# Light-part products over 128 zero-filled rows instead of 64 in a two-block transformer kernel

## The chip, the cores and the metric

The kernel runs on one core of one Trainium2 chip, as one launch. The metric is the device time of that launch in microseconds (us), as the median of three runs. All operands are in float32 in memory; the large products run in float32r passes on TensorE.

## The reference, cut to what matters

The reference is a chain of two blocks over 512 tokens of 1024 features (16 learned tokens are put ahead of them in the first block). Three places of it matter here.

- RWKV-7 time mixing: `w_log = -softplus(-(w0 + tanh(xw @ w1) @ w2)) - 0.5` and `a = sigmoid(a0 + (xa @ a1) @ a2)`. The latents `tanh(xw @ w1)` and `xa @ a1` have 64 features each.
- Stick-breaking attention over 16 heads of 64 features: `z = einsum('bhqd,bhkd->bhqk', q, k) * scale`, then `w = exp(log_sigmoid(z) + log_after)` for the valid keys, where `log_after` sums `log_sigmoid(-z)` over the keys between this one and the query, and then `w @ v`.
- Window attention with 16 query heads and 4 key-value heads of 64 features, over a band of 512 tokens and 256 context tokens: `s = einsum('bkgqd,bkjd->bkgqj', q, k) * hd**-0.5`, a masked softmax with a sink, and `p @ v`.

Around them stand two feed-forward layers per block, a short convolution and the norms; they take most of the time and aren't touched.

## The kernel before, in words

Everything is feature-major: features lie on the 128 partitions, tokens along the free axis. A float32 product is made of float32r products: an operand x is split in a heavy part (x rounded to float32r) and a light part (the rest), and `W.T x` becomes heavy times heavy, heavy times light, light times heavy. `Net.load_split` does this for weights (`whi` on ACT, L82, and `wlo` on DVE, L83), `Net.split` for data (L170 and L171, or L173 and L174 with a scale), and the loop of L131 issues the products of all dense layers.

Heads and latents have 64 features, so their operands fill half the partitions. The kernel stacks two parts there: one 128-row product covers heavy times heavy on 64 rows and light times heavy on the other 64. What is left, heavy times light, is a second product over the 64 rows of the head alone. This is the product the change touches, in three stages:

- `latents` (inside `rwkv`, L521 to L533): for 8 feature tiles, two latents and two halves of the tokens, a product over 128 rows (L529, operand `lh`) and one over 64 rows (L530, operand `ll`), then a Tanh on ACT into a tile of the pool `ew` and a store to DRAM. The steps alternate by hand with steps of `project` (L608), the projections.
- `scores` (inside `stick`, L1228): for each of 8 feature tiles, two heads and three PSUM banks, one to three regions of keys and queries; for each region a 128-row product and a 64-row product through the helper `mm` (L1223, `z<-qd,ks` and `z<-ql,ks`). DVE and ACT make the softplus of a bank; `weights` (also L1223, `s<-...`) sums it, `values` (L1294) multiplies with the values. The loop at L1347 runs 48 turns; scores are issued three turns ahead (AHEAD), and four steps of dense products, the generator `stream` with `project(j)` for the keys (`ev_k`), queries (`ev_q`) and values (`ev_v`) of the next feature tile, fill each turn. The query tiles `qd` and `ql` have one buffer.
- `softmax` (inside `window`, L1713): for 4 key-value heads and 4 query blocks, four heads with two products each over 128 rows (L1726) and 64 rows (L1727), 256 or 320 columns wide, in a PSUM tile `s` of a pool with two buffers. DVE takes the maximum (L1732) and a small minimum (L1734), ACT the exponential (L1736), which is the last reader of `s`. `values` (L1746) transposes and multiplies (L1753, L1762). Five steps of dense products (`fill`, `part`) are issued with each of the 16 turns.

Before that loop `window` makes keys and queries: `normed` (L1587) takes a projection, its mean square (L1593), the rotation (L1596, `t` on DVE in L1598, two POOL products L1599 and L1600), the inverse root (`Net.rsqrt`, L179 to L183, into `r`) and the last product by `r` (L1603). Its scratch comes from the pool `wq` with two buffers per tag; `ev_k` (L1606) then fills `kh` and `kl`, `ev_q` the stacked queries.

The order on each engine's queue is fixed when the program is built: the framework walks the instructions by priority (their order in the program) and by when its own estimates say their operands and buffers are ready, and adds the waits. A tile of a pool waits until the tile that had its buffer before has been read for the last time.

Of the kernel before, what the change touches and what calls it, by code (L numbers as in the profile page):

```python
"""Block of RWKV-7 and stick-breaking attention followed by a block of window attention and short convolution,
feature-major: features on partitions, tokens along the free axis."""
# [6 lines left out]
F32 = mybir.dt.float32  # L9
F32R = mybir.dt.float32r  # L10
BF16 = mybir.dt.bfloat16
AF = mybir.ActivationFunctionType
ALU = mybir.AluOpType
# [6 lines left out]
T1 = 528  # L20
# [7 lines left out]
class Vecs:  # L28
    """Column offsets of per-feature vectors packed as [128, n]."""
# [19 lines left out]
class Net:  # L49
# [18 lines left out]
    def load_split(self, srcs, n, shape=None):  # L68
        """Streams a weight chunk of n columns per partition and splits it in two float32r parts. It is one source, or
        with a shape (rows k of the partition) several, side by side."""  # L70
# [19 lines left out]
    def steps(self, xs, W, K, tiles, T, evac, gsz, psum, tag="slot", first=False, last=False):  # L90
        """Generator, a step for each 128 rows of W: out[tile] = W[:, tile].T @ x for 128-column tiles, in three float32r passes.
        T = 512: one bank per tile; otherwise the tokens lie as halves in two banks. With first, the first group
        takes the tokens in two halves, x(k, half); with last, the last one ends with one half, and evac gets
        (tile, psum, tokens)."""
# [4 lines left out]
        for gi, grp in enumerate(groups):  # L99
# [38 lines left out]
            # the halves of a tile are one group of a bank when both are open at once  # L138
# [20 lines left out]
    def squares(self, pool, name, names, tag="cst"):  # L159
        """Constant [128, 128] matrices by name."""  # L160
# [5 lines left out]
    def split(self, hi, lo, src, scale=None, bias=None):  # L166
        """hi + lo = src * scale + bias, both float32r."""
# [8 lines left out]
    def rsqrt(self, out, m, t):  # L176
        """out = m ** -0.5 with one Newton step; t is scratch."""
# [8 lines left out]
class Norm:  # L186
    """rs = 1/sqrt(mean square + eps) of each token, on all partitions, in two halves of the tokens. Squares are
    taken of src * weight where there are weights (columns of squared weights)."""
# [44 lines left out]
def halved(tc, T, mk, fill, prep=None):  # L233
    """x(k), x(k, half): the parts of operand k, made at their first use by fill(k, hi, lo, tokens)."""
# [22 lines left out]
def ffn1(net, l, h, skip):  # L257
    """Block 1: h += W_down(silu(gate) * val), causal conv of the up projection; h: 8 tiles of tokens, of which
    the first skip only feed the convolution (0: zeros precede the tokens)."""
# [65 lines left out]
R1, R2 = 0.58, 1.11  # L325
DENSE = (77, 90, 44, 38)
PAT = "cdpcddcpddcd"
# time of a side generator's wait, in units of its own
LAG = 1.57


# [1539 lines left out]
```

## Time and profile before

| what | value |
|---|---|
| median of 3 runs | 3076.61 us |
| lowest and highest | 3064.46 and 3077.65 us |
| span of the profiled execution, first to last instruction | 3064.8 us |
| TensorE (PE) busy | 2982.8 us, 97% |
| weight loads (PEld) busy | 2501.0 us, 82% |
| DVE, ACT, POOL busy | 1782.9, 1373.8, 372.6 us |

The profile shows one execution, of which no time outside its span is given; its span lies 11.8 us below the median of the runs and 0.3 us above the lowest. A matmul's busy time includes the tail in which the next one already runs, so the distance between the starts of two matmuls says what one costs in a stream, not its duration. PEld are the loads of the stationary operand, which are separate instructions. PEclk is the granted clock as a share of 2.4 GHz.

### The profile page before, as it was taken

To read this page: it belongs to the slowest core of one execution; us is meant where nothing else is said; L and a number is where in the kernel's file an instruction comes from. 1 tells how busy PE (TensorE), PEld (TensorE's weight loads), DVE (VectorE), ACT (ScalarE), POOL (GpSimd) and SP (SyncE) were. 2 spreads that over 40 slices of the span, in tenths; PEclk is the share of its full clock that TensorE was granted. 3 is DMA by queue.
4 is the path that set the end of the run, shared out by engine and by line. 5 is a ranking of instruction groups with operands and counts; after the bars stand their busy time and mean duration, and the time that the engine had idled before them with its cause. 6 is when DMAs were issued, how large, how long until landed. Compare 5 with 4: busy or idle time off the path is not lost.

```text
span 3064.8 us, 51007 instructions
## 1 busy us (share of the span) xinstructions
PE 2982.8 (97%) x21232; PEld 2501.0 (82%) x21232; DVE 1782.9 (58%) x2833; ACT 1373.8 (45%) x2416; POOL 372.6 (12%) x394
## 2 busy tenths in 40 slices
PE   6989999989999999999999999999999999999999
PEld 3877776779999988889999886668888888888888
DVE  6677557456664377675666377765555344365532
ACT  6554534444443267774443156554443232343431
POOL 2323324210000000000000111101111100101100
PEclk9999999989999999999999999999999999999999
DMA  4335456322222221112222331002232223223232
GB/s 132 124 111 157 156 185 197 112 91 83 90 91 90 85 70 45 46 42 90 90 90 90 96 108 56 21 8 69 90 97 93 93 90 94 92 90 95 91 100 86
DMA packets 269543, 286.28 MB, mean 93 GB/s; under 512 B 12384, under 2 KB 243936, under 8 KB 269312
## 3 DMA queue, kind: packets, MB, share of 16 engines
q1 hardware_dynamic: 269312, 283.03, 29.2%
q8 instruction: 166, 2.72, 0.4%
q14 instruction: 65, 0.53, 0.1%
HBM read 271.70 MB, written 11.29 MB: 92 GB/s over the span
## 4 chain that ended last, share of the span: by engine, by line
PE 76%; DVE 1%; ACT 1%; issue 0%; DVEq 0%; ACTq 0%
PE slot L131 65%; PE z L1223 2%; PE s L1223 1%; PE s L1727 1%; PE po L1762 1%; PE pt L1753 1%; PE s L1726 1%; PE po L1294 1%; PE psn L215 1%; PE s L1729 1%; PE psh L1593 0%; PE psr L1596 0%; ACT whi L82 0%; PE psd L1768 0%; DVE wlo L83 0%
## 5 line engine op out<-in xcount | busy, mean ns | idle before, releaser
L131 PE MATMUL slot<-xh,whi 128*128 128x264 f32 (+3 forms) x2848 | 783.7, 324 | 2.6 <-ACT xh L1439 1.9
L131 PE MATMUL slot<-xh,wlo 128*128 128x264 f32 (+3 forms) x2848 | 777.0, 322 | 1.4 <-DVE wlo L83 1.4
L131 PE MATMUL slot<-xl,whi 128*128 128x264 f32 (+3 forms) x2848 | 777.4, 321 | 0.7 <-DVE xl L1440 0.7
L82 ACT ACTIVATE whi<-raw 128x1024 fp32r<-128x1024 f32 x368 | 382.6, 1040 | 830.2 <-PE slot L131 700.8
L83 DVE TENSOR_TENSOR wlo<-raw,whi 128x1024 fp32r<-128x1024 f32 x368 | 447.9, 1218 | 511.1 <-ACT whi L82 507.2
L131 PEld LDWEIGHTS slot<-xh,whi 128*128 128x128 f32 x2848 | 481.1, 189 | 54.4 <-issue 8.7
L131 PEld LDWEIGHTS slot<-xl,whi 128*128 128x128 f32 x2848 | 482.4, 190 | 44.4 <-issue 1.5
L131 PEld LDWEIGHTS slot<-xh,wlo 128*128 128x128 f32 x2848 | 480.8, 189 | 45.0 <-DVE wlo L83 1.6
L131 PE MATMUL slot<-mh,whi 128*128 128x512 f32 (+2 forms) x1012 | 291.0, 327 | 0.8 <-DVE h L1489 0.5
L131 PE MATMUL slot<-ml,whi 128*128 128x512 f32 (+2 forms) x1012 | 291.3, 327 | 0.0
L131 PE MATMUL slot<-mh,wlo 128*128 128x512 f32 (+2 forms) x1012 | 291.1, 327 | 0.0
L200 POOL TENSOR_TENSOR acc<-acc,sq 128x512 f32<-128x512 f32 (+2 forms) x40 | 67.0, 1674 | 1130.9 <-ACT sq L205 743.5
L131 PEld LDWEIGHTS slot<-mh,whi 128*128 128x128 f32 x1012 | 173.9, 188 | 19.9 <-DVE h L1489 0.9
L131 PEld LDWEIGHTS slot<-mh,wlo 128*128 128x128 f32 x1012 | 174.1, 189 | 18.2
L131 PEld LDWEIGHTS slot<-ml,whi 128*128 128x128 f32 x1012 | 173.6, 188 | 18.1
L1478 POOL TENSOR_TENSOR t<-t 128x512 f32<-128x512 f32 x44 | 75.3, 1711 | 460.9 <-DVE t L1456 425.0
L289 DVE TENSOR_TENSOR u<-slot,rs 128x528 f32<-128x528 f32 (+1 forms) x88 | 61.6, 702 | 109.0 <-PE slot L131 108.1
L170 ACT ACTIVATE mh<-t 128x512 fp32r<-128x512 f32 (+1 forms) x88 | 55.6, 632 | 145.5 <-POOL t L1478 78.8
L608 PE MATMUL slot<-xl,whi 128*128 128x264 f32 x384 | 110.0, 306 | 10.2 <-DVE xl L582 6.1
L608 PE MATMUL slot<-xh,whi 128*128 128x264 f32 x384 | 117.3, 326 | 1.4 <-ACT V L611 0.7
L608 PE MATMUL slot<-xh,wlo 128*128 128x264 f32 x384 | 106.5, 298 | 0.0
L171 DVE TENSOR_TENSOR ml<-t,mh 128x512 fp32r<-128x512 f32 (+1 forms) x88 | 60.9, 694 | 57.5 <-ACT mh L170 55.7
(415 smaller groups left out, 4889.2 us busy)
## 6 DMA issues: line engine op xcount, KB each, us to landing
aw<-in_ada_w SPq DMA_DIRECT2D x96, 512.0 KB, 3.9
raw<-in_ffn_up SPq DMA_DIRECT2D x88, 512.0 KB, 3.5
raw<-in_ffn_w_up SPq DMA_DIRECT2D x80, 512.0 KB, 3.4
raw<-in_ffn_down SPq DMA_DIRECT2D x40, 512.0 KB, 3.4
raw<-in_ffn_w_down SPq DMA_DIRECT2D x40, 512.0 KB, 3.4
raw<-in_sc_w_in SPq DMA_DIRECT2D x20, 512.0 KB, 3.4
raw<-in_win_w_qkv SPq DMA_DIRECT2D x12, 512.0 KB, 3.6
h<-in_xT SPq DMA_DIRECT2D x16, 264.0 KB, 4.6
```

Of the source, the lines that this page charges most:

```text
L82: nc.scalar.activation(hi[:, :n], raw[:, :n], AF.Copy)
L83: nc.vector.tensor_tensor(lo[:, :n], raw[:, :n], hi[:, :n].bitcast(F32), op=ALU.subtract)
L131: self.nc.tensor.matmul(out(j, i), a, b if i is None else b[:, i * H:i * H + H], start=(k == 0 and p == 0 and not (i and shared)), stop=(k ...
L170: nc.scalar.activation(hi, src, AF.Copy)
L171: nc.vector.tensor_tensor(lo, src, hi.bitcast(F32), op=ALU.subtract)
L200: nc.gpsimd.tensor_tensor(self.acc, self.acc, sq, op=ALU.add)
L215: add = lambda a, **kw: nc.tensor.matmul(ps[:, :N], self.net.ones, a, **kw)
L289: nc.vector.tensor_tensor(u[:, 2:].rearrange("p (a t) -> p a t", a=2), p, rs3, op=ALU.mult)
L608: nc.tensor.matmul(s[:, :264], a[:, c], b[:, halves[hf]], start=k == n == 0, stop=k == 7 and n == 2)
L1223: nc.tensor.matmul(out, a, x, **kw)
L1294: nc.tensor.matmul(po[hp(e), lo:hi], vt[:, b, hp(e)], w(e)[:, c + lo - t0:c + hi - t0], start=B == 0 and b == 2, stop=B == 2 and hi == 512)
L1478: nc.gpsimd.tensor_tensor(t, t, gate[j], op=ALU.mult)
```

## The change

Each 64-row product becomes a product over all 128 rows. The heavy operand with both stacked parts is already there on 128 rows; the light operand gets a tile of its own per head with zeros on the other 64 partitions, written by POOL memsets, so that the sum is the same.

- `latents`: `ll` becomes two tiles, one of them new, with a memset of 64 x 528 each.
- `stick`: `ql` becomes [128, 2, 516] with two memsets of 64 x 516 for each feature tile. The scratch `kf` of `ev_k` and `ev_q` goes from two buffers to one.
- `window`: `kl` becomes four tiles instead of two, with four memsets of 64 x 768. In `normed` the tag `r` is gone: `r` takes its buffer from the tag `hr`, which the rotation's `t` uses too.

```diff
-        ll, gh, gl, g3 = (room[:, i] for i in range(4))
+        gh, gl, g3 = (room[:, i] for i in range(3))
+
+        ll = [room[:, 3], tp.tile([128, T1], F32R, name="ll")]
         for r in range(2):
-            net.split(lh[r][hp(r)], ll[hp(r)], lat[hp(r)])
+            nc.gpsimd.memset(ll[r][hp(1 - r)].bitcast(F32), 0.0)
+            net.split(lh[r][hp(r)], ll[r][hp(r)], lat[hp(r)])
             nc.scalar.activation(lh[r][hp(1 - r)], lat[hp(r)], AF.Copy)
...
-                        nc.tensor.matmul(s[:, :264], w2[r][hp(r), js], ll[hp(r), c], start=False, stop=True)
+                        nc.tensor.matmul(s[:, :264], w2[r][:, js], ll[r][:, c], start=False, stop=True)
...
-            kf = t2.tile([128, T1], F32, tag="kf", name="kf")
+            kf = t2.tile([128, T1], F32, tag="kf", name="kf", bufs=1)
...
-            qf = t2.tile([128, T1], F32, tag="kf", name="qf")[:, :TQ]
+            qf = t2.tile([128, T1], F32, tag="kf", name="qf", bufs=1)[:, :TQ]
             qd = t2.tile([128, 2, TQ], F32R, tag="qd", name="qd", bufs=1)
-            lo = t2.tile([128, TQ], F32R, tag="ql", name="ql", bufs=1)
+
+            ql = t2.tile([128, 2, TQ], F32R, tag="ql", name="ql", bufs=1)
             nc.vector.tensor_tensor(h3(qf), p, h3(rs[:, Q0:]), op=ALU.mult)
             for e in range(2):
                 own, other = hp(e), hp(1 - e)
-                net.split(qd[own, e], lo[own], qf[own], 0.125)
+                net.split(qd[own, e], ql[own, e], qf[own], 0.125)
                 nc.scalar.activation(qd[other, e], qf[own], AF.Copy, scale=0.125)
-            ops["q", j] = (qd, lo)
+                nc.gpsimd.memset(ql[other, e].bitcast(F32), 0.0)
+            ops["q", j] = (qd, ql)
...
-                mm(z[:, c:c + w], ks[hp(e), e, kb], ql[hp(e), q], start=False, stop=True)
+                mm(z[:, c:c + w], ks[:, e, kb], ql[:, e, q], start=False, stop=True)
...
-        kl = [big.tile([128, 768], F32R, name=f"kl{i}") for i in range(2)]
+        kl = [big.tile([128, 768], F32R, name=f"kl{i}") for i in range(4)]
...
+        for i, t in enumerate(kl):
+            nc.gpsimd.memset(t[hp(1 - i % 2)].bitcast(F32), 0.0)
...
-            s, sq, m, r = (wq.tile([128, T2], F32, tag=t, name=t)[:, :T] for t in ("hq", "sq", "m", "r"))
+
+            s, sq, m = (wq.tile([128, T2], F32, tag=t, name=t)[:, :T] for t in ("hq", "sq", "m"))
...
             nc.vector.tensor_scalar(m, ps[:, :T], 1.0 / 64, 1e-6, op0=ALU.mult, op1=ALU.add)
+            r = wq.tile([128, T2], F32, tag="hr", name="hr")[:, :T]
             net.rsqrt(r, m, sq)
...
-                    nc.vector.tensor_tensor(kl[t][hp(e), d], n[hp(e), c], k[hp(e), d].bitcast(F32), op=ALU.subtract)
+                    nc.vector.tensor_tensor(kl[2 * t + e][hp(e), d], n[hp(e), c], k[hp(e), d].bitcast(F32), op=ALU.subtract)
...
-                    nc.tensor.matmul(o, q[r, qc], kl[kvh // 2][r, ks], start=False, stop=not mk)
+                    nc.tensor.matmul(o, q[:, qc], kl[kvh][:, ks], start=False, stop=not mk)
```

## Rows read from the trace of the kernel before

**Rows 1.** The head of the profile's page: the span, then busy time, share and instructions of each engine.

```profile
span 3064.8 us, 51007 instructions
PE 2982.8 (97%) x21232; PEld 2501.0 (82%) x21232; DVE 1782.9 (58%) x2833; ACT 1373.8 (45%) x2416; POOL 372.6 (12%) x394
```

**Rows 2.** Busy time by stretch. A row has the stretch (us from the span's start), its length, then busy us and number of instructions of PE, PEld, DVE, ACT and POOL, the granted clock, the share of the DMA engines and GB/s. The first row is the stretch of the latents and the second a part of it, then the stick-breaking attention, the start of the window attention, and the window attention's loop.

```profile
58.00:95.00 37.00, 35.65 (x149) 25.80 (x149) 11.18 (x14) 23.62 (x51) 5.24 (x5) 0.82 0.35 124
60.00:73.00 13.00, 13.00 (x40) 9.58 (x41) 6.55 (x7) 9.87 (x20) 4.04 (x3) 0.50 0.29 104
...
1091.00:1365.00 274.00, 273.96 (x1888) 234.44 (x1887) 191.11 (x330) 201.00 (x353) 3.07 (x13) 0.99 0.16 46
1820.00:1866.00 46.00, 39.74 (x188) 30.33 (x187) 37.56 (x53) 34.11 (x64) 11.90 (x8) 0.93 0.26 77
1866.00:2075.00 209.00, 208.55 (x1114) 132.00 (x1114) 142.77 (x308) 116.92 (x262) 23.85 (x27) 1.00 0.07 21
```

**Rows 3.** The light-part products of the three stages, from the views of their lines: number, shortest, median and longest duration in ns, first and last start, rows x columns of the stationary operand, shapes of the moving one.

```profile
L530 PE MATMUL slot<-room x32: 279/385/586, 59.0 to 94.6; 64*128 64x264 f32 x32
...
L1223 PE MATMUL z<-ql,ks x96: 268/386/699, 1092.0 to 1350.3; 64*128 64x272 f32 x16, 64*128 64x144 f32 x16, 64*128 64x16 f32 x16, 64*128 64x400 f32 x16
...
L1727 PE MATMUL s<-kl,q x128: 378/394/413, 1866.9 to 2073.1; 64*128 64x256 f32 x64, 64*128 64x320 f32 x64
```

**Rows 4.** PE in order of time, dense products alone: first start, time to the last end, engine, line, operation, tile, shapes and number. Six of 512 columns in a row, then a row of products of 264 columns, two per entry; of each series the first and the last.

```profile
1922.51 0.39 PE L131 MATMUL slot<-xh,whi 128*128 128x512 f32 x1
...
1923.67 0.40 PE L131 MATMUL slot<-xh,wlo 128*128 128x512 f32 x1
...
1203.29 0.41 PE L131 MATMUL slot<-xl,whi 128*128 128x264 f32 x2
...
1205.23 0.28 PE L131 MATMUL slot<-xh,whi 128*128 128x264 f32 x1
```

**Rows 5.** PE in order of time in the window attention: a pair of 320 columns and what follows it, then one of 256 columns and what follows it.

```profile
1899.72 0.39 PE L1726 MATMUL s<-kh,q 128*128 128x320 f32 x1
1900.04 0.41 PE L1727 MATMUL s<-kl,q 64*128 64x320 f32 x1
1900.39 0.23 PE L1729 MATMUL s<-masks 128*128 128x128 bf16 x1
...
1924.46 0.36 PE L1726 MATMUL s<-kh,q 128*128 128x256 f32 x1
1924.75 0.38 PE L1727 MATMUL s<-kl,q 64*128 64x256 f32 x1
1925.06 0.38 PE L1726 MATMUL s<-kh,q 128*128 128x256 f32 x1
```

**Rows 6.** The weight loads (PEld) in order of time in the same attention; in brackets the idle time before the load and what ended it.

```profile
1901.63 0.18 PEld L1727 LDWEIGHTS s<-kl,q 64*128 64x128 f32 x1 [0.15 <-issue]
```

**Rows 7.** PE in order of time in the stick-breaking attention: the first product of a unit of bank 0 (three pairs) and the product after the unit, the same for a unit of bank 1 (two pairs) and of bank 2 (one pair).

```profile
1201.36 0.39 PE L1223 MATMUL z<-qd,ks 128*128 128x272 f32 x1
...
1202.94 0.39 PE L131 MATMUL slot<-xh,whi 128*128 128x264 f32 x1
...
1146.47 0.45 PE L1223 MATMUL z<-qd,ks 128*128 128x400 f32 x1
...
1147.62 0.38 PE L131 MATMUL slot<-xl,whi 128*128 128x258 f32 x1
...
1150.52 0.48 PE L1223 MATMUL z<-qd,ks 128*128 128x512 f32 x1
...
1151.35 0.40 PE L131 MATMUL slot<-xh,whi 128*128 128x258 f32 x1
```

**Rows 8.** PE in order of time in the latents: the first of two pairs and the product after them.

```profile
83.29 0.28 PE L529 MATMUL slot<-room 128*128 128x264 f32 x1
...
84.45 0.39 PE L608 MATMUL slot<-xh,whi 128*128 128x264 f32 x1
```

**Rows 9.** Two heads of the window attention in order of time: the first score product on PE and the exponential on ACT that reads the same PSUM tile last.

```profile
1931.14 0.39 PE L1726 MATMUL s<-kh,q 128*128 128x256 f32 x1
...
1934.10 0.69 ACT L1736 ACTIVATE P<-s,st 128x512 f32<-128x512 f32 x1 [0.41 <-DVE st L1734]
...
1938.30 0.71 PE L1726 MATMUL s<-kh,q 128*128 128x320 f32 x1
...
1944.42 0.80 ACT L1736 ACTIVATE P<-s,st 128x640 f32<-128x640 f32 x1 [2.20 <-DVE st L1734]
```

**Rows 10.** ACT, DVE and PE in order of time at the start of the window attention, for a pair of key tiles and then a pair of query tiles: the second tile's write of `r`, the first tile's last read of its `r`, and the next wait of PE.

```profile
1830.84 0.63 ACT L179 ACTIVATE r<-m 128x512 f32<-128x512 f32 x1 [0.43 <-DVE m L1601]
...
1835.23 0.68 DVE L1603 TENSOR_TENSOR hq<-hq,r 128x512 f32<-128x512 f32 x1
...
1844.03 0.39 PE L131 MATMUL slot<-ch,whi 128*128 128x256 f32 x1 [3.30 <-ACT whi L82]
...
1851.32 0.63 ACT L179 ACTIVATE r<-m 128x512 f32<-128x512 f32 x1
...
1856.08 0.68 DVE L1603 TENSOR_TENSOR hq<-hq,r 128x512 f32<-128x512 f32 x1
...
1858.55 0.53 PE L131 MATMUL slot<-ch,wlo 128*128 128x256 f32 x1 [2.10 <-DVE wlo L83]
```

**Rows 11.** POOL: a memset by form (number, busy us, mean ns of one, idle us before them and what ended it), and its longest wait in the stick-breaking attention (us in total, times, longest).

```profile
L710 POOL MEMSET w<- 128x448 f32 x4 | 1.9, 475 | 5.4 <-PE slot L544 5.3
...
POOL vf L1185 <- PE psv L1197: 158.4, 7, 31.0
```

More of the change, by code (lines that the diff above doesn't have):

```diff
@@ L1713, in softmax @@
         def softmax(kvh, b):
-            qc, w, r = slice(b * 128, b * 128 + 128), NK[b] // 2, hp(kvh % 2)
+            qc, w = slice(b * 128, b * 128 + 128), NK[b] // 2
             st = at.tile([128, 16], F32, name="st")
```

## The prediction

> **What bounds the kernel now.** I read the head of the page first. TensorE is busy 97% of a span of 3064.8 us, and the next engine, DVE, 58% [rows 1]; the reader is to see that anything that shortens PE's stream shortens the run, unless another engine steps into its place in the stage concerned. So the second view is the busy time by stretch, for the three stages that hold the touched products. In the stick-breaking attention PE is busy 273.96 of 274 us, in the window attention 208.55 of 209, in the latents 35.65 of 37 [rows 2]. The third view gives what is touched: 32, 96 and 128 light-part products over 64 rows, 256 in all; the third shape list leaves out one form, the 16 products of 512 columns and 16 of 4 columns, which the code gives (BANKS) [rows 3].
>
> Busy time does not tell what one product costs, so the fourth view is PE in order of time, for the distance from start to start. In the dense layers five distances of 512-column products take 1923.67 - 1922.51 = 1.16 us, 0.232 each, and sixteen of 264 columns take 1.94 us, 0.121 each [rows 4]. The line through both has (0.232 - 0.121) / 248 = 0.00045 us for a column, which makes 0.117 for 256 columns, 0.125 for 272, 0.146 for 320 and 0.182 for 400. A heavy product of 320 columns that is followed by a 64-row one takes 0.32 us to the next start, and the 64-row one 0.35 to the 128-row product behind it [rows 5]: both more than twice the 0.146. The weight loads say why: the load of a 64-row product starts only after 0.15 us of idle time that no semaphore ends, at 1901.63, together with its product [rows 6], while dense products at 0.121 us apart must have theirs loaded ahead. So I take it that each change of the number of rows, to 64 and back, breaks the stream and costs some 0.17 to 0.2 us.
>
> **The change part by part.** The 64-row products become 128-row ones of the same columns between 128-row neighbours. The columns are the same, so I price both products of a pair at the dense distance.
>
> Window attention: a pair of 320 columns takes 0.67 us from its start to the next one's, and will take 2 x 0.146 = 0.29: 0.38 less, 64 times 24.2 us. A pair of 256 takes 0.60, then 0.23: 0.37 less, 64 times 23.4 us [rows 5]. Sum 47.6 us. Stick-breaking attention, by units: bank 0 takes 1.58 us for three pairs and will take 2 x 0.125 + 4 x 0.121 = 0.73 (nothing narrower than 264 columns is credited with less than 0.121), 0.85 less; bank 1 takes 1.15, then 2 x 0.182 + 2 x 0.121 = 0.61, 0.54 less; bank 2 takes 0.83, then 0.46, 0.37 less [rows 7]. With 16 units of each that is 16 x 1.76 = 28.1 us. Latents: two pairs take 1.16 us, then 4 x 0.121 = 0.48, 0.34 less for each pair, 32 times 10.8 us [rows 8]. That stretch runs for 13 us at a granted clock of 0.50, the 1.2 GHz level [rows 2]; the pairs there cost more, and I leave that out. The whole saving on PE's queue is 47.6 + 28.1 + 10.8 = 86.5 us.
>
> What of it reaches the end depends on the engines that now have room. The highest share of a stretch at which I see a helping engine run while PE waits for it is DVE's 37.56 of 46 us, 0.82, at the start of the window attention [rows 2]; I use it as a ceiling. Window loop: DVE's 142.77 us at 0.82 need 174 us, so the gain there lies between 209 - 174 = 35 and 47.6. A second limit of that stage is its PSUM tile `s`: a head holds it from its first product to the end of its exponential, 1934.79 - 1931.14 = 3.65 us in the short case and 1945.22 - 1938.30 = 6.92 in the long one [rows 9]. With two buffers and 64 heads the stage can't be shorter than 64 x 3.65 / 2 = 117 or 64 x 6.92 / 2 = 221 us; the middle hold of 5.3 us gives 169, a gain of 40, which is also near the middle of the first pair of bounds. I take 40. Stick-breaking: ACT's 201 us at 0.82 need 245, a gain of up to 29, more than the 28.1, so I take 28. Latents: ACT's 23.62 us at 0.82 need 28.8 of 37, a gain of 8.2; between that and 10.8 I take 9.5. Together 77.5 us.
>
> The added parts. POOL gets 2 memsets of 528, 16 of 516 and 4 of 768 columns. A memset of 448 columns takes 0.475 us [rows 11]; by proportion these take about 0.56, 0.55 and 0.81, together 1.1 + 8.8 + 3.3 = 13 us on an engine that is busy 12% [rows 1]. I cost them at nothing: they wait for the same buffer as DVE's write of the light part, and run beside the four ACT and two DVE instructions with which `ev_q` splits the queries. Without that cover two memsets, 1.1 us, would stand before the first score of each of 8 feature tiles, 8.8 us. Behind them on POOL's queue wait the memsets of `vf` and `ks`, of which the score loop has its own reserve (scores three turns ahead). The single buffer of `kf` makes `ev_q` wait until `ev_k` has read its own; between the two stand 8 dense steps of 6 products, 48 x 0.121 = 5.8 us [rows 4]. I cost it at nothing; were `ev_k` later than that, the wait would be its remaining splits, which no row here prices.
>
> The shared tag `hr` costs something. With two buffers for `t` and `r` together, `t` and `r` of one call fill both, so the second of two calls in a row can't write its `r` before the first has read its own for the last time. In the key pair that write began at 1830.84, and the last read ended at 1835.91; in the query pair 1851.32 and 1856.76 [rows 10]. That puts the second tile 5.1 and 5.4 us later. Behind the write wait, on ACT, the splits of the keys and then `whi`, on DVE `wlo`, and for these PE already waits 3.30 and 2.10 us [rows 10]. The cost lies between 0 (other work is placed ahead) and 10.5 us; the first tile's splits can go ahead of the second's in either pair, so I take 6, a little over the middle. Later calls stand alone, a turn or more apart, and cost nothing.
>
> Sum: 77.5 - 6 = 71.5 us less. The profiled span would go from 3064.8 to 2993 us; that execution shows no time outside its span, which lies 11.8 us below the median, at the lowest run. Against the median the forecast is 3076.6 - 71.5 = 3005 us.
>
> One rule of the Trainium skill speaks against this. TensorE: Matmul & The Clock Gate, in the section Part 3: Packing small matmuls — row/col tiling, says that a weight load runs beside a product in flight only where their row groups differ. By that, a full-height product could never hide its load, and the change would gain nothing: 3083 us by the third rival's working, instead of 3005. The dense products of rows 4 have the same full height and stand 0.121 us apart, so this trace doesn't bear the rule out.
>
> **The rivals.** First, the window loop meets its two PSUM buffers. For it speaks the long hold of 6.92 us, and that DVE has 142.77 us of work in that stage; against it that the short hold is 3.65 [rows 2, 9]. If the mean hold goes to 6.1 us the stage takes 64 x 6.1 / 2 = 195 us, a gain of 14 in place of 40, and the time is 3031 us.
>
> Second, all of the saving arrives, and the denser stream of the latents also holds the full clock. The stretch 60 to 73 us is all PE work at half clock [rows 2]; its 8 or so pairs save at least 8 x 0.34 = 2.7 us, and the 10 us that are left would take 5 at the full clock. Then 86.5 + 5 = 91.5 us go, and with no cost of `hr` the time is 2985 us.
>
> Third, the change doesn't do what it says: the delay belongs to the load itself and stays for a product of 128 rows. Then pairs cost what they do, the `hr` cost of 6 us is added, and the time is 3083 us, no change by measure. Against it stand rows 4.
>
> Fourth, slower: the memset of `ql` stands on POOL's queue behind the memset of `vf`, which waits up to 31.0 us for the transposes of the values, 158.4 us over 7 tiles [rows 11], and the first light product of each tile waits for it. At 158.4 us in full the time is 3005 + 158 = 3163 us; it decides from (71.5 + 15.4) / 7 = 12.4 us a tile. Against it: `ev_q` comes before `ev_v` in `project`, and the scores are issued three turns later.
>
> **How the numbers follow.** Forecast 0.66 (a gain between 50 and 85 us, 2992 to 3027), first rival 0.20, second 0.07, third 0.04, fourth 0.03. The time is that of the forecast, 3005 us. The range reaches down to the second rival's 2985 less a little for the spread of the runs, of which the lowest was 12 us below the median: 2982. Upward it reaches the first rival's 3031: 3032. Half a percent, 15 us, is about what a measurement of this kernel can tell from no change. Faster: forecast, second rival and nearly all of the first, 0.92; same: the third and the rest of the first, 0.05; slower: 0.03.
>
> **What the profile would show.** The light products at L530, L1223 and L1727's successors with 128 rows, 0.15 us from a 320-column start to the next instead of 0.32 and 0.35, and no idle time before their loads: if those distances stay, the third rival is right. The window loop at about 169 us, the stick-breaking attention at 246, the latents at 27 to 28. If PE shows waits for `s` behind ACT's exponential or DVE's maximum, the first rival is at work. PE's two waits at the start of the window attention grow by some 3 us each, behind `whi` and `wlo`. POOL memsets of 0.55 us that no score waits for. The prediction is wrong if the waits of that start grow by tens of us, or if DVE above 0.9 of the window loop shows that my ceiling is too low.

## The result and the profile after

The changed kernel takes 2993.0 us (median of 4 runs, 2986.3 to 3013.2) against 3077.1 us of the kernel before (median of 4 runs, 3064.5 to 3091.1; three of them are those of the section on time). The ratio is 0.973, with a 95% interval of 0.969 to 0.977: 84 us less by the medians, 69 to 97 by the interval. The forecast was 3005 us in a range of 2982 to 3032. A second series later gave 2993.0 against 3073.6 us, a ratio of 0.974 (0.970 to 0.978).

The head of the page after, which answers [rows 1]: the span, then busy time, share and instructions of each engine.

```profile
span 2984.5 us, 51034 instructions
PE 2895.0 (97%) x21232; PEld 2468.6 (83%) x21232; DVE 1779.0 (60%) x2833; ACT 1367.5 (46%) x2416; POOL 385.7 (13%) x416
```

TensorE executes the same 21232 products and is busy 88 us less; its share stays at 97%, so it is still what bounds the kernel. POOL has the 22 added memsets. Busy time by stretch, with the columns of [rows 2]: the latents, the stick-breaking attention, and the window attention's loop.

```profile
60.50:86.10 25.60, 22.73 (x154) 21.75 (x155) 10.66 (x13) 22.23 (x51) 4.88 (x6) 0.87 0.51 180
1074.00:1317.00 243.00, 242.90 (x1890) 224.26 (x1888) 189.94 (x330) 198.15 (x353) 10.07 (x27) 1.00 0.18 52
1818.90:2003.00 184.10, 180.05 (x1167) 126.73 (x1166) 142.21 (x313) 119.19 (x272) 23.89 (x28) 1.00 0.08 24
```

The light products of the three stages, as in [rows 3] (of the latents, the half that the trace names so):

```profile
L533 PE MATMUL slot<-ll,room x16: 280/286/422, 62.1 to 84.3; 128*128 128x264 f32 x16
...
L1228 PE MATMUL z<-ql,ks x96: 251/280/394, 1075.0 to 1302.3; 128*128 128x272 f32 x16, 128*128 128x144 f32 x16, 128*128 128x16 f32 x16, 128*128 128x400 f32 x16
...
L1735 PE MATMUL s<-kl,q x128: 276/303/364, 1819.0 to 1992.6; 128*128 128x256 f32 x64, 128*128 128x320 f32 x64
```

The median light product of the window loop got shorter, from 394 ns to 303, with twice the rows. That is less than the gain of a pair; the rest lies in the distances between starts. PE in order of time in the window loop, which answers [rows 5]: one head of 320 columns in each half, from the light product of its first half to the mask product of its second.

```profile
1881.72 0.31 PE L1735 MATMUL s<-kl,q 128*128 128x320 f32 x1
1881.87 0.23 PE L1737 MATMUL s<-masks 128*128 128x128 bf16 x1
1881.91 0.39 PE L1734 MATMUL s<-kh,q 128*128 128x320 f32 x1
1882.13 0.31 PE L1735 MATMUL s<-kl,q 128*128 128x320 f32 x1
1882.29 0.23 PE L1737 MATMUL s<-masks 128*128 128x128 bf16 x1
```

A light product now takes 1881.87 - 1881.72 = 0.15 us to the next start, where it took 0.35. The heavy one takes 1882.13 - 1881.91 = 0.22, where it took 0.32 and the forecast had 0.146; e3 comes back to it. The same view in the other two stages: a unit of bank 0 of the stick-breaking attention, its first and last product and the products after the unit, which answers the first part of [rows 7]; then two pairs of the latents and the product after them, which answer [rows 8].

```profile
1195.11 0.29 PE L1228 MATMUL z<-qd,ks 128*128 128x272 f32 x1
...
1195.60 0.26 PE L1228 MATMUL z<-ql,ks 128*128 128x16 f32 x1
1195.71 0.49 PE L131 MATMUL slot<-xh,whi 128*128 128x264 f32 x2
1196.04 0.41 PE L131 MATMUL slot<-xl,whi 128*128 128x264 f32 x2
...
70.82 0.28 PE L532 MATMUL slot<-room 128*128 128x264 f32 x1
70.94 0.28 PE L533 MATMUL slot<-ll,room 128*128 128x264 f32 x1
71.07 0.28 PE L532 MATMUL slot<-room 128*128 128x264 f32 x1
71.19 0.29 PE L533 MATMUL slot<-ll,room 128*128 128x264 f32 x1
71.31 0.41 PE L611 MATMUL slot<-xh,whi 128*128 128x264 f32 x2
```

The three pairs shown take 0.60 us. Units of bank 0 come in two kinds by turns: those behind a wide product, as this one, went from 1.47 to 0.61 us, those behind narrow products, as the one in [rows 7], from 1.58 to 0.71. Two pairs of the latents take 0.49 us where they took 1.16.

The table cuts each run into stages by the first and last starts of the products that mark them, in us: the latents up to the gates, the rest of the first mixing layer with how much of it ran at the half clock (granted 0.50, the 1.2 GHz level), the stick-breaking attention, the start of the window attention from the context's norm to the first score, and its loop. What is not shown agrees within some 1 us a stage between all runs, apart from the first product of the latents, which starts at 57.7 to 61.7 us.

| kernel | latents | rest of mixing layer | of it at half clock | stick | window start | window loop |
|---|---|---|---|---|---|---|
| before | 37.3 | 583.7 | 35.9 | 273.6 | 62.4 | 216.2 |
| after | 25.7 | 576.6 | 16.0 | 242.3 | 63.0 | 183.2 |
| e1_light_adjacent | 37.2 | 587.1 | 49.5 | 270.9 | 63.3 | 196.7 |
| e2_shared_scratch | 40.0 | 580.5 | 32.2 | 273.7 | 63.7 | 217.1 |
| e3_after_no_masks | 25.5 | 585.0 | 39.0 | 242.2 | 64.3 | 179.1 |
| e4_memsets_fourfold | 25.7 | 606.5 | 92.1 | 247.7 | 63.3 | 183.2 |
| e5_latents_only | 25.8 | 585.3 | 46.2 | 270.8 | 63.3 | 216.2 |
| e6_stick_only | 37.2 | 580.7 | 34.1 | 242.3 | 62.5 | 216.5 |
| e7_window_only | 52.0 | 577.2 | 17.3 | 270.9 | 64.4 | 183.2 |
| e8_after_again | 25.6 | 576.9 | 15.8 | 242.3 | 63.2 | 183.2 |
| e9_gates_128 | 25.9 | 575.7 | 23.9 | 242.3 | 63.3 | 183.2 |
| e10_ada_pairs | 25.6 | 576.4 | 20.4 | 242.3 | 66.2 | 183.2 |

The span fell by 80.3 us: latents 11.6, rest of the mixing layer 7.1, stick 31.3, window loop 33.0, less 0.6 at the start of the window attention and 2.0 by the later start. The stick's 273.6 us hold a stretch of 6.8 us at half clock at their beginning; the kernels with the same stage that lack it (e1, e5, e7) take 270.9, so the change is worth 28.6 there. The 7.1 us of the mixing layer are clock too. A straight line through the eleven kernels of the table whose products there keep their order (all but e10) makes that stage 0.39 us longer for each us at half clock, or 0.32 without e4; the unchanged latents of e2 and e7, with 20.5 and 49.8 us at half clock against 13.7 before, give 0.40. At 0.39 the 19.9 us of half clock less are worth 7.8 us, and nothing of the 7.1 is left for the change.

### The profile page after: what moved, and what is told of

Same layout as the page of the kernel before. It is cut to its first block, busy times and chain, and to the rows that moved or that the text cites. A ratio compares the mean times of both kernels' runs of the same rounds, so it can differ in the third digit from the quotient of the medians.

```text
span 2984.5 us, 51034 instructions
## 1 busy us (share of the span) xinstructions
PE 2895.0 (97%) x21232; PEld 2468.6 (83%) x21232; DVE 1779.0 (60%) x2833; ACT 1367.5 (46%) x2416; POOL 385.7 (13%) x416
## 4 chain that ended last, share of the span: by engine, by line
PE 74%; DVE 2%; ACT 1%; issue 0%; POOL 0%; DMA 0%; DVEq 0%; ACTq 0%
PE slot L131 65%; PE s L1228 1%; PE po L1770 1%; PE z L1228 1%; PE pt L1761 1%; PE po L1299 1%; PE psn L215 1%; PE s L1734 1%; PE s L1735 0%; ACT whi L82 0%; PE psh L1600 0%; POOL hq L1607 0%; DVE wlo L83 0%; DVE st L1740 0%; PE psd L1776 0%
## 5 line engine op out<-in xcount | busy, mean ns | idle before, releaser
L131 PEld LDWEIGHTS slot<-xl,whi 128*128 128x128 f32 x2848 | 481.2, 189 | 44.9 <-issue 2.5
```

The lines of the kernel that those rows point to most:

```text
L131: self.nc.tensor.matmul(out(j, i), a, b if i is None else b[:, i * H:i * H + H], start=(k == 0 and p == 0 and not (i and shared)), stop=(k ...
```

## The experiments

**Change of height or short product: e1_light_adjacent.** It is the kernel before with the four products of a head in another order, still over 64 rows; the edit in short form:

```
-    mm heavy(0); mm light(0); masks(0); mm heavy(1); mm light(1); masks(1)
+    mm heavy(0); mm heavy(1); mm light(0); mm light(1); masks(0); masks(1)
```

> The kernel before, with the four score products of a head of the window attention in another order: both 128-row products, then both 64-row products, then the masks. The number of 64-row products stays, the changes of height are halved. If a change of height is what costs (theory), a head saves two of its four breaks, about 0.37 us, 64 times 24 us: the stretch from the first score to the last product of the values goes from 216.7 us to about 193, and the first of two adjacent 64-row products of 320 columns takes about 0.15 us to the next start. If a 64-row product is slow by itself, or no load of the same rows can be hidden (rival), the distance stays at 0.32 or more and the stretch at 217 us.

Measured: the window loop went from 216.2 to 196.7 us, 19.5 less, without one product changed. PE and PEld in order of time for one head of 320 columns:

```profile
1932.93 0.45 PE L1723 MATMUL s<-kh,q 128*128 128x320 f32 x2
1933.31 0.56 PE L1729 MATMUL s<-kl,q 64*128 64x320 f32 x2
1933.80 0.29 PE L1732 MATMUL s<-masks 128*128 128x128 bf16 x2
```

```profile
1932.93 0.19 PEld L1723 LDWEIGHTS s<-kh,q 128*128 128x128 f32 x1
1933.31 0.29 PEld L1729 LDWEIGHTS s<-kl,q 64*128 64x128 f32 x2 [0.19 <-issue]
1933.80 0.11 PEld L1732 LDWEIGHTS <-masks 128*128 128x128 bf16 x2 [0.19 <-issue]
```

PEld idles 0.19 us at the change to 64 rows and again at the change back, and the first load behind a change starts together with its product. Two neighbouring 64-row products take 0.49 us for the pair, where each cost 0.35, together 0.70, between 128-row neighbours [rows 5]. From one light start to the other it is 0.25 us (mean of 30). So the price goes with the number of changes, while the number of 64-row products is the same, which is the reason the forecast gave. The new order does one more thing: it takes the mask product away from in front of 40 heavy products (16 have one there, 56 had). By the 0.084 us that e3 finds for that, some 3.4 of the 19.5 us are the masks' (an estimate), and 16 are left for the changes of height. The 0.25 is more than the 0.15 of dense products: the second load starts 0.107 us behind the first (two loads of 0.188 end in 0.29), and the first product, which itself began only as its load did, does not hide it. So the loop gained less than the 24 us of the theory.

**The shared scratch: e2_shared_scratch.** The kernel before with the tag alone.

```
-            s, sq, m, r = (... for t in ("hq", "sq", "m", "r"))
+            s, sq, m = (... for t in ("hq", "sq", "m"))
...
+            r = wq.tile([128, T2], F32, tag="hr", name="hr")[:, :T]
```

> The kernel before, with the root's tile r taking its buffer from the tag hr as in the change, and nothing else of it. The prediction's step says 6 us (0 to 10.5) more between the first product of the context's norm and the first score of the window attention, 62.4 us before: about 68 us, with PE's waits for whi and wlo there longer. Rival: other work is placed into the gap and the stretch stays within 1 us of 62.4.

Measured: the start of the window attention goes from 62.4 to 63.7 us, and kernels without the edit (e1, e5, e6) take 62.5 to 63.3 there; the loop is 0.9 us longer. That stretch too holds half clock, 3.4 us in e2 and 9.9 to 12.3 in the other four, so e2 alone may hide up to some 3 us of cost. The better pair is e7, the window's part with the tag (64.4 us, 11.8 of them at half clock), against e1 and e5 without it (63.3, 12.2 and 12.3): the tag costs about 1 us, not 6. The waits of PE in that stretch (total, times, longest), first before, then e2, then after:

```profile
PE slot L131 <- ACT whi L82: 3.3, 1, 3.3
PE slot L131 <- DVE wlo L83: 2.9, 2, 2.1
```

```profile
PE psh L1593 <- ACT sq L1590: 4.3, 2, 2.5
PE slot L131 <- DVE wlo L83: 2.2, 4, 1.2
PE slot L131 <- ACT whi L82: 1.8, 2, 1.5
```

```profile
PE psh L1600 <- ACT sq L1597: 2.8, 2, 2.6
PE slot L131 <- DVE wlo L83: 2.1, 4, 1.2
PE slot L131 <- ACT whi L82: 0.8, 2, 0.5
```

The waits behind `whi` and `wlo` did not grow, they fell from 6.2 to 4.0 and 2.9 us, and a wait for the square of the next tiles (`sq`) came in their place, which the kernel before does not have. ACT in order of time in e2 shows both, for the second key tile: its `r`, a `whi`, its first split, and the square of the next tile.

```profile
1833.69 0.63 ACT L179 ACTIVATE hr<-m 128x512 f32<-128x512 f32 x1 [4.37 <-POOL hq L1600]
...
1838.90 1.04 ACT L82 ACTIVATE whi<-raw 128x1024 fp32r<-128x1024 f32 x1
...
1842.28 0.42 ACT L1614 ACTIVATE kh<-hq 64x256 fp32r<-64x256 f32 x1 [2.34 <-DVE hq L1604]
...
1845.64 0.57 ACT L1590 ACTIVATE sq<-slot 128x512 f32<-128x512 f32 x1
```

Counted from the start of the stage, the second `r` is written at 30.7 us and not at 26.6, the second tile's splits begin at 39.3 and not at 35.2, and the square behind them at 42.6 and not at 40.6; but the first of the two `whi` that stood behind those splits, at 38.7, is now ahead of them, at 35.9 (the other went from 39.7 to 44.9). What the second `r` waits for is POOL's sum L1600, the last reader of the rotation's `t`.

**The short mask products: e3_after_no_masks.** The changed kernel without the 96 mask products.

```
-        MK = [[(1, 2)], [(0, 1), (4, 2)], [(0, 1), (4, 2)], [(2, 1)]]
+        MK = [[], [], [], []]
```

> The kernel after the change without the 96 mask products of the window attention, so the window is not applied: the masked keys count in the softmax. After the change the stretch from the first score to the last product of the values takes 183.7 us instead of the forecast 177, and a 128-row product of 320 columns right behind a mask takes 0.23 us to the next start, not 0.146. Theory: the loads of the two products behind so short a product come too late; without masks the distances fall to 0.146, which is about 80 x 0.084 + 96 x 0.04 = 10 us, and the stretch goes to about 173 us. Rival: DVE and the PSUM buffers of the scores bound that loop; then the stretch stays at 181 to 184 us and PE waits for them instead.

Measured: loop 183.2 to 179.1 us, 4.1 less, between the two. In order of time, the second pair of a head without masks and what follows it:

```profile
1890.70 0.31 PE L1734 MATMUL s<-kh,q 128*128 128x320 f32 x1
1890.85 0.31 PE L1735 MATMUL s<-kl,q 128*128 128x320 f32 x1
1891.00 0.38 PE L1761 MATMUL pt<-cst,P 128*128 128x128 f32 x2
```

Behind a light product the heavy one takes 0.146 us on the mean (36 of 320 columns), which is the price of the forecast; behind a mask product it takes 0.230 in the kernel after (45 of them; 0.202 with 256 columns, 19). PEld of the kernel after shows why, for the head shown in the section on the result:

```profile
1881.86 0.10 PEld L1737 LDWEIGHTS <-masks 128*128 128x128 bf16 x1
1881.87 0.20 PEld L1734 LDWEIGHTS s<-kh,q 128*128 128x128 f32 x1
1881.99 0.19 PEld L1735 LDWEIGHTS s<-kl,q 128*128 128x128 f32 x1
```

The mask product takes 0.04 us to the next start, less than the 0.107 to 0.12 us that two loads are apart. The heavy product's load begins only at 1881.87, with the mask product and not ahead of it, and the light one's 0.12 us behind that, while the light product starts at 1882.13. That this row of loads is the delay is read from the two views; that the delay goes with the mask is measured. The mask product differs from its neighbours in its type too (bf16), and e3 takes away both, but the kernel after settles which it is: in its stick-breaking attention a dense product of 264 columns right behind a float32r product of 16 or 4 columns takes 0.206 us to the next start (21 of them, 0.203 to 0.209), where 0.121 is the dense distance [rows 4]. The two products that start at 1195.71 in the section on the result are such a pair: 0.33 us together, where two dense ones take 0.24. So it is the short product. 64 heavy products with a light one behind them stand right behind a mask, and 15 behind a transpose take as long; at 0.230 - 0.146 = 0.084 us that is 6.6 us of the forecast's saving that did not come. But without masks the loop gains 4.1 us only. The waits for the tile `s` (total, times, longest), in the loops of before (PEld alone has one), after and e3 in turn, and for after also PE's longest wait in that loop:

```profile
PEld s L1726 <- ACT P L1736: 0.8, 4, 0.2
```

```profile
PE pt L1761 <- ACT PT L1764: 2.1, 3, 0.9
PE s L1734 <- ACT P L1744: 1.4, 3, 0.6
```

```profile
PE s L1734 <- ACT P L1744: 5.6, 8, 1.3
```

PE's own wait grew by 4.2 us: what the masks gave up, the two PSUM buffers of `s` partly took back. The first rival's wait is real in this loop, and small at the size of this change (1.4 us on PE).

**The memsets of `ql`: e4_memsets_fourfold.** The changed kernel with each of these memsets done four times.

```
-                nc.gpsimd.memset(ql[other, e].bitcast(F32), 0.0)
+                for _ in range(4):
+                    nc.gpsimd.memset(ql[other, e].bitcast(F32), 0.0)
```

> The kernel after the change with each memset of the light queries of the stick-breaking attention done four times in a row: 48 more memsets of 516 columns, some 26 us of POOL's time. If they are covered (theory), the stretch from the first score to the last product of the values stays at 242 us within 1 us. If the first score of a tile waits for them (rival), each of 8 tiles is late by up to 3.3 us and the stretch goes to up to 268 us.

Measured: the stick stage takes 247.7 us, 5.4 more, and the wait appears in e4 that the changed kernel does not have (waits in the stick stage, of PE and PEld in e4, then the two waits of POOL in the kernel after):

```profile
PEld z L1229 <- POOL ql L1215: 5.4, 7, 1.0
PE z L1229 <- POOL ql L1215: 3.9, 7, 0.8
```

```profile
POOL vf L1188 <- PE psv L1200: 132.5, 7, 26.1
POOL ql L1214 <- PE z L1228: 78.9, 7, 11.4
```

A memset took 0.524 us (forecast 0.55). At two a tile (1.05 us) nothing of it is seen, at eight (4.2 us) 5.4 / 7 = 0.77 us of each tile's are: the cover ends at about 3.4 us. The total of 3022.5 us is not to be read as a price of memsets: that execution has 92 us at half clock in the first mixing layer.

**Each part alone: e5_latents_only, e6_stick_only, e7_window_only.** The kernel before with the change's lines in one stage.

```
e5  +  ll = [room[:, 3], tp.tile([128, T1], F32R, name="ll")]
    -  nc.tensor.matmul(..., w2[r][hp(r), js], ll[hp(r), c], ...)
    +  nc.tensor.matmul(..., w2[r][:, js], ll[r][:, c], ...)
e6  -  mm(..., ks[hp(e), e, kb], ql[hp(e), q], ...)
    +  mm(..., ks[:, e, kb], ql[:, e, q], ...)       (with the kf/qf buffer and memsets)
e7  -  nc.tensor.matmul(o, q[r, qc], kl[kvh // 2][r, ks], ...)
    +  nc.tensor.matmul(o, q[:, qc], kl[kvh][:, ks], ...)   (with the tag hr and memsets)
```

> The kernel before with the latents' part of the change alone. Theory: each part's gain is its own stage's, so the stretch from the first product of the latents to the first of the gates goes from 37.3 us to 25.7 as with the whole change, the rest of the first mixing layer (583.7 us before, 576.6 after) shows no gain of its own beyond its stretches of half clock, and the two attentions stay at 273.6 and 216.2 us. Rival: the 7 us of the rest are a gain that the earlier latents bring, and come again here with as much half clock as before.

> The kernel before with the stick-breaking attention's part of the change alone. Theory: the stretch from the first score to the last product of the values goes from 273.6 us to about 242, all other stretches stay but for half clock; latents 37.3, window loop 216.2. Rival: part of the 31 us came from the other parts of the change, and the stretch stays over 247.

> The kernel before with the window attention's part of the change alone, the shared tag hr with it. Theory: the loop goes from 216.2 us to about 183, its start stays within 2 us of 62.4, the stick-breaking attention at 273.6, the latents at 37.3. Rival: the loop's 33 us hang on what came before it, and it ends elsewhere by more than 3 us.

Measured: each moves its own stage to the value it has in the changed kernel, and no other: latents 25.8 us, stick 242.3, loop 183.2. The parts add up, and neither the latents' denser stream nor the stick's changes a later stage. The totals were 3055.5, 3032.3 and 3042.4 us; that of e7 holds 50 us at half clock in its latents, which it has unchanged.

**Do 96 rows cost as 64 do: e9_gates_128.** The changed kernel with the gates' 96-row products brought to 128 rows with zeros.

```
-    pairs = (g2h, gh), (g2h, gl), (g2l, gh), (g23[0:96], g3[0:96])
+    pairs = (g2h, gh), (g2h, gl), (g2l, gh), (g23, g3)
```

> The kernel after the change, with the 16 products of the gate latents that take 96 rows made 128 rows high too (rows 96 to 127 of both operands zero). If a change of height costs its two breaks whatever the height (theory), each of the 16 gives back 0.3 to 0.37 us, 5 to 6 us in all, where PE is the bound: the stretch of the rest of the first mixing layer gets shorter by 3 to 6 us at equal half clock, and the distance from a 96-row product of 264 columns to the next falls from about 0.31 to 0.12 us. If 96 rows stand closer to 128 than 64 do (rival), the distance before is already near 0.12 and nothing moves.

Measured: the distances do not move. The 96-row products never cost anything; a row of the kernel after, with the products before and behind it:

```profile
86.37 0.28 PE L547 MATMUL slot<-room,g2l 128*128 128x264 f32 x1
86.49 0.29 PE L547 MATMUL slot<-room,g 96*128 96x264 f32 x1
86.62 0.41 PE L547 MATMUL slot<-room,g2h 128*128 128x264 f32 x2
```

It stands 0.12 and 0.13 us from its neighbours, as dense products do [rows 4]. On the mean of the 16 it is 0.124 us to the next start with 96 rows and 0.122 with 128. The stage is 575.7 us with 23.9 at half clock against 576.6 with 16.0, which at 0.39 us each is 4 us less, as the theory had it; but 3.4 of these lie in a wait of PE for `h` in the output projection, 4.3 us in the kernel after and 0.9 in e9, and not in the products. So "each change of the number of rows" was too wide: 64 beside 128 rows breaks the stream, 96 beside 128 does not.

**The same kind of change elsewhere: e10_ada_pairs.** e9 with the ada products (four blocks of 32 columns) issued for two rows of weights at a time, so that the stream enters and leaves that form half as often.

```
-    for q in range(4): matmul(ps[32 * q:32 * q + 32], sc[:, k], w[...], ...)
+    if k % 2 == 0: w0 = w
+    for kk, ww in ((k - 1, w0), (k, w)) if k % 2 else ():
+        for q in range(4): matmul(ps[32 * q:32 * q + 32], sc[:, kk], ww[...], ...)
```

> The kernel after the change with 128-row gate products and with the modulation products of the first mixing layer (four products of 32 columns side by side, 768 in all) issued eight at a time instead of four. A group of four leaves 0.31 us to the next product of another shape and costs 0.15 to 0.21 us on the way in. If every change between tile shapes costs as it does for the 64-row products (theory), half of some 140 groups less gives 10 to 20 us in the rest of the first mixing layer, about 563 us without half clock, and 2975 to 2985 us in all. Rival: that layer waits on the chain of its recurrence or on the weight buffers that now fill in pairs, and gains nothing or loses up to 20 us.

Measured: no gain is shown. The runs of such products fell from 118 to 77, and sixteen together take 1.00 us (311.29 to 312.29 us) where eight take 0.57 in the kernel after. That is 2 x 0.57 - 1.00 = 0.14 us for a run that goes, 41 x 0.14 = 5.7 us in all by estimate, less than the 10 to 20 expected. Of this the layer shows little: it takes 576.4 us with 20.4 at half clock, against 575.7 with 23.9 in e9, of which it is an edit, and 576.9 with 15.8 in e8; at 0.39 us each it is 2 us longer than the one and 2 us shorter than the other. PE waits 30.2 us there, against 24.0 in e9 and 28.3 in e8, so part of the saving went into waits, which the busy share of PE does not tell. The median of 4 runs is 3000.0 us against 2993.0 of e8, a ratio to the kernel before of 0.977 (0.972 to 0.981); three of the four ran at a mean clock of 0.985, and the fourth took 2989.0 us at 0.992, where e8 took 2988.7 and 2987.9 at 0.991 and 0.993.

**How much is clock: e8_after_again.** The changed kernel, unedited, beside the kernel before.

> The changed kernel as it is, for its granted clock in more runs. The forecast's own gain is 71.5 us, the median of the first runs 84. Theory: the difference is half clock that falls into the first mixing layer in some runs and not in others, so the runs of this kernel spread over 10 us or more with the mean granted clock (about 3 us longer for each 0.001 less between 0.98 and 0.995), and at equal clock the two kernels are 70 to 75 us apart. Rival: the change itself shortens that layer, and the two stay 80 us or more apart at equal clock.

Measured, with the granted clock of each execution as a mean over its span: 2987.9 us (0.993), 2999.1 (0.989), 2997.2 (0.989), 2988.7 (0.991) against 3064.0 (0.989), 3080.1 (0.983), 3062.4 (0.989), 3080.9 (0.983), 3080.8 (0.984), 3073.6 (0.986), 3060.9 (0.990). Three executions of each kernel have 0.989 (with 2996.0 of the first series, and 3064.9 beside e5): means of 2997.4 and 3063.8 us, 66 us apart. All 17 runs with a clock on record (eight of after, nine of before) say more: two straight lines with one slope, 2.3 us for each 0.001 of mean clock, lie 69 us apart, with a standard error of 1.3. So at equal clock the kernels differ by some 66 to 72 us (two standard errors); the rival's 80 is out, and the theory's 70 to 75 is met at its lower end. The median clocks, 0.986 for these runs before and 0.990 for the eight after, make another 9 us at that slope. The rest of the 81 to 84 us between the medians is within the scatter of the runs.

## Why the prediction was right

The time came 12 us below the forecast and inside the range. The cause was right; that the sum fits so well is in part luck, since wrong terms cancel. By its steps:

**The cause.** Right. Rows of 64 between rows of 128 broke the stream; e1 shows that the price goes with the number of changes, and the distances of 0.15 and 0.12 us that the changed kernel has none. The third rival (the load itself) is out. The rule of the Trainium skill, TensorE: Matmul & The Clock Gate, section Part 3: Packing small matmuls — row/col tiling, by which a full-height product could not hide its load if the sentence is taken alone, does not hold in this trace: pairs of full height stand 0.12 us apart, and a light product's load starts at 1881.99, beside the heavy product of 1881.91 and 0.14 us ahead of its own. The same section of the Trainium skill has another way to load ahead, into a background weight buffer, which fits these rows and which the forecast did not name.

**Stick-breaking attention: forecast 28, measured 28.6.** By units, the three banks take 0.66, 0.56 and 0.56 us on the mean behind the first feature tile (from 1.53, 1.11 and 0.84): 0.86, 0.54 and 0.28 less, where the forecast had 0.85, 0.54 and 0.37. The last was 0.09 too much. All units together gained 26.9 us (56.3 in e5, which lacks the half clock, to 29.4); another 2.3 came from the 45 dense products right behind a unit, 10.3 us in e5 and 8.0 after, which the forecast left out. So the 28 fits because one term was too large and one was missing. The ceiling of 0.82 for ACT was met as it happens: 198.15 of 243 us.

**Latents: forecast 9.5, measured 11.6.** On the low side because of the half clock. The stage had 13.7 us at 0.50 before and 6.8 after; at the 0.40 us of e2 and e7 that is worth 2.8 us, which the forecast had left out of its sum and put into its second rival. At equal clock the gain is 8.8. ACT was busy 22.23 of 25.6 us, 0.87, so the ceiling of 0.82 did not hold either.

**Window loop: forecast 40, measured 33.** The step that failed is the price of the heavy product. Both products of a pair were priced at the dense distance, 47.6 us together; the sums of their start distances in the loop went from 39.2 to 26.6 us (heavy) and from 41.8 to 18.0 (light), 36.4 less. The row that gave 0.32 us for a heavy product stood behind a mask product, and of the 0.32 the change of height had only 0.322 - 0.230 = 0.09; the other 0.084 belongs to the short product ahead, as e3 shows, and stays: 6.6 us over 79 products. Of the 4.6 us that are left of the difference (47.6 - 36.4 = 11.2), 2.9 lie in the 30 heavy products that stand beside other shapes (0.55 us behind the 512-column products L1600 and L1603, for one) and 1.2 in light ones. That the loop itself fell by 33.0 and not 36.4 is in the dense products and the transposes of the same loop, whose distances to the next start grew by 4.3 us in sum. Of these, 2.9 are waits of PE behind ACT, which grew for `s` from 0 to 1.4 us and for the transposes' tile `pt` from 0.5 to 2.1. The ceilings of the forecast did not decide: DVE is at 142.21 of 184.1 us, 0.77, under the 0.82, and PE waits for `s` 1.4 us. The bound of 221 us from the long hold could not have been one, since the loop before took 216. So the 40 was cut from 47.6 for a limit that did not bind, where the price itself was too high.

**The tag `hr`: forecast 6, measured about 1.** The step from "the second tile's `r` comes 5 us later" to "the splits behind it come later" held for the second key tile, whose splits came 4.0 us later in e2; the next step, that `whi` comes later behind them, failed for the one that PE had waited for, since it was placed ahead of them. The statement that PE's two waits there would grow by 3 us each is wrong: they fell, and the wait for the square of the next tiles, 4.3 us in e2 and 2.8 in the changed kernel, came in their place. What the second `r` waited for was POOL's sum with `t`, and not the first tile's last read of `r`.

**The memsets and the buffer of `kf`: forecast 0, measured 0**, with the cover of the memsets measured in e4. The fourth rival is out.

**The sum.** 28.6 + 11.6 + 33.0 - 0.6 = 72.6 us against 71.5: the errors of the window loop (7 too much gain) and of `hr` (5 too much cost) and the latents (2 too little gain) cancel, which is luck. Less the latents' 2.8 us of clock it is 69.8, and the runs at equal clock are 69 us apart. The 84 us between the medians hold some 11 us more than the sum, most of it clock: stretches of 16 to 92 us at the half level in the first mixing layer, which differ from run to run and from kernel to kernel. Whether the change itself makes them rarer is not settled: the clocks of after lie between 0.980 and 0.994 and those of before between 0.983 and 0.990.

## What to carry to other kernels

Look for products of 64 rows between products of 128 in a TensorE-bound stream and compare the distance from start to start with that of dense neighbours; zero-filled rows took no time on TensorE in these runs, and each change of height that goes away is worth 0.09 to 0.19 us here. Where the rows cannot be filled, put the products of the same height side by side: that gave 19.5 of the loop's 33 us, some 3.4 of them by moving the masks. Behind a short product (128 columns of bf16, 16 columns of float32r) price the next one 0.08 us above the dense distance.

## What the runs showed of the hardware

- 96 rows next to 128 cost nothing (0.12 and 0.13 us to the neighbours, e9), while a 64-row product of 320 columns next to 128-row ones costs 0.09 us ahead of it (0.322 against 0.230, means of heavy products behind a mask) and 0.19 behind it (0.342 against 0.149).
- Behind a change of height the first load starts only with its product, and the next one 0.107 us later, so the second product of a 64-row pair comes after 0.25 us and not 0.15 (e1).
- A product of 320 columns behind a 128-column mask product takes 0.23 us, behind a full one 0.146 (e3); one of 264 columns behind a float32r product of 16 or 4 columns takes 0.206, behind a full one 0.121 (after).
- Of the half clock (0.50 granted), the profiled executions had between 38 us (after) and 120 (e4) in all. At 0.39 us each, the price in the first mixing layer, this one quantity makes a run 15 to 47 us longer (an estimate). A stretch of e4 shows PE busy throughout while it lasts:

```profile
529.60:587.60 58.00, 58.00 (x546) 40.96 (x545) 15.03 (x37) 12.38 (x37) 3.06 (x7) 0.50 0.15 47
```
